# A decoder trunk in three blocks: where the sample group's expert rows are gathered, and who makes the weights' low parts

## The chip, the cores and the metric

The kernel runs on one core of one Trainium2 chip. The metric is the device time of one execution in microseconds; lower is better. The engines are named as the profile names them: PE is TensorE, DVE is VectorE, ACT is ScalarE, POOL is GpSimd, SP is SyncE, which here only issues transfers.

## What is computed

One layer of a decoder, for a prompt of 1024 rows and a sample group of 64 rows (8 sequences of 8 steps), with the same weights for both. Cut to what matters:

```
xn = RMSNorm(x)
lru_x, lru_gate, q, k, v, gate_lru, gate_attn = split(xn @ w_in)
A = (RG-LRU(conv4(lru_x)) * gelu(lru_gate)) @ w_branch_lru
B = window_attention(norm(q), norm(k), v) @ w_branch_attn
h = x + (sigmoid(gate_lru) * A + sigmoid(gate_attn) * B) @ w_out
y = h + PEER(RMSNorm(h))
```

PEER chooses, for each row, 8 heads x 16 experts of 16384 (the best sums of two lists of 128 key scores). An expert e is one row u[e] and one row v[e] of 1024 numbers each: the result is the sum over the 128 chosen experts of gelu(x . u[e]) * g[e] * v[e], with g a softmax of the scores.

## The kernel before

**Blocks.** The rows pass through the trunk in three blocks, called here by the number that the code gives them: block 0 is prompt rows 0 to 255 and the sample group, block 1 is prompt rows 256 to 639, block 2 is prompt rows 640 to 1023. `trunk` runs one block: the query, key and value columns (`qkv`, which makes columns 4 and 0 of the next block ahead of time), `attention`, a first merge of eight steps (`w_branch_attn`), the recurrent stage (`lru`, six calls), a second merge of eight steps (`w_branch_lru`), the output columns (`w_out`, four calls), the second norm, and `retrieve`, which makes the query columns and the 16 best keys of each list (16 calls).

**Weights in two parts.** Every weight is used as a sum of a high part (the fp32 value rounded to TensorE's fp32r) and a low part (what is left), and three matmuls make one product (`mm3`, L183 to L185). The weights come in 84 chunks of 128 x 1024 numbers (0.524 MB) and are loaded anew in each block. For each chunk ACT writes the high part into `whi` and DVE subtracts it for the low part, `wlo` (`split`, L163 and L164). `wsplit` (L201) counts the uses of a chunk. At the first use, in block 0, POOL sends the low part to memory (`lo_d`, L213). At the second the low part is subtracted again. At the third, SP reads it back (L209) and nothing is subtracted. There are three `whi`, three `wlo` and three `wraw` buffers, and SP's transfers are issued in one order: what stands behind a transfer that waits for a buffer waits too.

**Work in the background.** What follows a block's retrieval is a generator, `behind(b)`, that the next block's trunk advances: `bg(n)` takes n steps from it, and the tuples PG1 (while block 1 runs) and PG2 (while block 2 runs) say how many at each kind of call. Their eight entries belong to the first merge, the recurrent stage, the second merge, the output columns, the norm, the query columns, the q/k/v columns, and the score groups of attention. At the end of a block `bg(1000)` takes all that is left. A background is made of three kinds of steps:

- *choice steps* (`choose`): for each 128 rows, the best of the pairs of keys, the experts' numbers and the softmax, on DVE; the sample group comes first, and its experts' numbers and weights go to the small buffer `est` (L851);
- *gather steps*, for the sample group alone: its 64 rows x 128 experts are laid out as 128 partitions x 64 slots. `early_u` gathers one u row a partition for a slot (POOL, L963) and multiplies it by x (DVE, L965); after 64 slots comes a gelu. `early_v` gathers v rows (L978) and adds them up (L983); then the two halves and the residual are added, and the sample group's y is written;
- *g building* (`build_g`): for each 4 rows a 128 x 128 table of weights, as a product of two one-hot tables (DVE L940 and L941, ACT L943, PE L923), copied by ACT into `sg` (L924); 8 steps fill one `sg`, and SP writes it (L926). Block 0 has 64 such steps, block 1 has 96.

In the loop of `behind`, each step takes one choice step and, once the sample group's choice is there and attention is past, one gather step: of u behind block 0 (while block 1 runs), of v behind block 1 (while block 2 runs). g building comes after both.

**One large buffer.** Attention's keys and values (`at`), the gathers (`et`: x or the sum, and three rows) and g building's `sg` are all tiles of one tag, `at`, that has a single buffer. A tile takes it when the one before has been used for the last time.

**Order.** The program is written out in the order of the code, and a planner then places the instructions on each engine by the order of the code and by when it reckons them ready, so background work is interleaved with the trunk's and can run later, or a little earlier, than its place in the code.

After the blocks comes the expert loop for prompt rows (`dense`), which takes more than half of the time and is not touched.

Of the kernel before, what the change touches and what calls it, by code (L numbers as in the profile page):

```python
# [58 lines left out]
NR = 3  # L59
GBL = 1  # L60
PG0 = (0, 0, 0, 0, 0, 0, 0, 0)
PG1 = (5, 5, 4, 5, 2, 2, 0, 0)
PG2 = (6, 6, 5, 1, 2, 4, 2, 2)
LATE = 3
VJ = 1
EARLY = (4, 0)
# [4 lines left out]
def f32(ap):  # L71
    return ap.bitcast(F32)


class Kern:
# [125 lines left out]
    def wsplit(self, key, hi, lo, raw):  # L201

        nc = self.nc
        m = self.chunk.setdefault(key, len(self.chunk))
        use = self.uses[key] = self.uses.get(key, 0) + 1
        kept = self.lo_d[m].rearrange("p (k c) -> p k c", c=raw.shape[2])
        if use == 3:
            nc.scalar.copy(hi, raw)
            nc.sync.dma_start(f32(lo), kept)  # L209
            return  # L210
        self.split(hi, lo, raw)
        if use == 1:
            nc.gpsimd.dma_start(kept, f32(lo))  # L213

    def load_c(self, src, c0):

# [79 lines left out]
    def trunk(self, bi, x, raw, bg):  # L296
# [4 lines left out]
        xh, xl = x  # L301
        self.pg = (PG0, PG1, PG2)[bi]
        self.at_free = False
# [688 lines left out]

    def behind(self, b):

        early, left = None, True
        ch = self.choose(b)
        while left or early is not False:
            if early is None and self.es is not None and self.at_free:
                early = self.early_v() if b else self.early_u()
            if left:  # L1000
                left = next(ch, None) is not None
            if early and next(early, None) is None:
                early = False
            yield True
        for _ in self.build_g(b):
            yield True
# [203 lines left out]
```

## Time and profile before

| what | value |
|---|---|
| runs | 3771.19 us median of 3 (3761.95 to 3776.55) |
| the profiled execution | 3777.02 us; its span, from the first to the last instruction, 3775.2 us |
| mean granted TensorE clock of that execution | 0.945 of full speed |
| PE, DVE, ACT, POOL busy | 3401.7, 2889.4, 1453.8, 1539.4 us |

The profile is of one execution, and times in it are microseconds from the start of its span. A PE that is busy is not PE at its peak, since matmuls overlap; the time of a stage is read from the stretch between its first and last instruction, and its limit from the engine that is full there or from what the others wait for.

### The profile page before, as it was taken

How to read it: one execution, taken by the hardware profiler on the slowest of the kernel's cores; microseconds unless marked ns; L12 is line 12 of the kernel's file. 1: busy time of each engine (PE TensorE's matmuls, PEld its weight loads, DVE VectorE, ACT ScalarE, POOL GpSimd, SP SyncE). 2: the span in 40 equal slices, each digit the busy share in tenths (PEclk: the TensorE clock that was granted, in tenths of full speed). 3: DMA queues.
4: the chain of work that ended last, by engine and by line, in shares of the span. 5: the costliest groups of instructions: out<-in, count | busy, mean ns of one | idle time of the engine just before them, and what ended most of it. 6: DMA issues, size and time to landing. Idle time of an engine off the chain costs nothing. (4 is left out here: it accounts for less than half of the span.)

```text
span 3775.2 us, 59354 instructions
## 1 busy us (share of the span) xinstructions
PE 3401.7 (90%) x21891; PEld 3244.8 (86%) x21891; DVE 2889.4 (77%) x6727; ACT 1453.8 (39%) x2969; POOL 1539.4 (41%) x1240
## 2 busy tenths in 40 slices
PE   6898999868898998769779999999999999999996
PEld 6798978758795887668679999999999999999995
DVE  6567797998689975546999777777777776778777
ACT  4555345445854473676222222222222222222220
POOL 0011100340000222000367676767667776777774
PEclk8899999879998999889789999999999999999998
DMA  7388833776552899645478898989989899899897
GB/s 229 108 260 283 264 97 96 242 231 220 183 187 69 272 320 344 238 159 199 162 259 285 314 311 289 312 298 321 311 298 319 307 316 312 310 320 318 310 310 276
DMA packets 539235, 968.36 MB, mean 257 GB/s; under 512 B 38108, under 2 KB 356508, under 8 KB 535840
## 3 DMA queue, kind: packets, MB, share of 16 engines
q0 software_dynamic: 141120, 513.86, 38.1%
q1 hardware_dynamic: 397824, 450.70, 37.5%
q8 instruction: 172, 2.82, 0.3%
q14 instruction: 119, 0.97, 0.1%
HBM read 860.10 MB, written 105.99 MB: 256 GB/s over the span
## 5 line engine op out<-in xcount | busy, mean ns | idle before, releaser
L183 PE MATMUL ou<-ah,vh 128*128 128x256 f32 (+1 forms) x2048 | 637.0, 315 | 58.7 <-DVE dac L1078 30.5
L183 PE MATMUL sc<-dx,uh 128*128 128x256 f32 (+1 forms) x2048 | 636.6, 311 | 11.0 <-DMA gt<-g_d 8.7
L185 PE MATMUL sc<-dx,ul 128*128 128x256 f32 (+1 forms) x2048 | 635.4, 311 | 1.3 <-POOL ul L164 1.3
L184 PE MATMUL sc<-dx,uh 128*128 128x256 f32 (+1 forms) x2048 | 636.2, 311 | 0.0
L184 PE MATMUL ou<-al,vh 128*128 128x256 f32 (+1 forms) x2048 | 632.0, 311 | 3.5 <-DVE al L164 3.2
L185 PE MATMUL ou<-ah,vl 128*128 128x256 f32 (+1 forms) x2048 | 630.3, 310 | 2.5 <-POOL vl L164 2.5
L903 DVE SCALAR_TENSOR_TENSOR acc<-row,hv,acc 128x1024 f32<-128x1024 f32 x384 | 493.6, 1285 | 147.7 <-DMA row<-in_expert_v,iA 145.5
L891 DVE SCALAR_TENSOR_TENSOR row<-row,xt 128x1024 f32<-128x1024 f32 x384 | 464.9, 1216 | 133.6 <-DMA row<-in_expert_u,iA 126.3
L889 POOL DMA_INDIRECT row<-in_expert_u,iA x384 | 366.4, 954 | 279.5 <-DVE row L891 193.2
L901 POOL DMA_INDIRECT row<-in_expert_v,iA x384 | 360.8, 940 | 273.3 <-DVE acc L903 189.9
L183 PEld LDWEIGHTS ou<-ah,vh 128*128 128x128 f32 x2048 | 387.5, 190 | 77.9 <-DVE dac L1078 40.3
L164 POOL TENSOR_TENSOR ul<-un,uh 128x1024 fp32r<-128x1024 f32 x128 | 308.0, 2406 | 330.2 <-DMA gt<-g_d 303.4
L183 PEld LDWEIGHTS sc<-dx,uh 128*128 128x128 f32 x2048 | 392.0, 191 | 12.2 <-ACT uh L163 9.0
L184 PEld LDWEIGHTS ou<-al,vh 128*128 128x128 f32 x2048 | 389.3, 190 | 6.0 <-DVE al L164 5.4
L185 PEld LDWEIGHTS sc<-dx,ul 128*128 128x128 f32 x2048 | 390.9, 191 | 2.1 <-POOL ul L164 2.1
L184 PEld LDWEIGHTS sc<-dx,uh 128*128 128x128 f32 x2048 | 391.9, 191 | 0.0
L185 PEld LDWEIGHTS ou<-ah,vl 128*128 128x128 f32 x2048 | 388.4, 190 | 2.7 <-POOL vl L164 2.7
L1078 DVE TENSOR_TENSOR dac<-dac,ou 128x384 f32<-128x384 f32 (+1 forms) x672 | 314.9, 482 | 46.0 <-PE ou L185 44.9
L163 ACT CAST uh<-un 128x1024 fp32r<-128x1024 f32 x128 | 134.5, 1051 | 496.3 <-PE sc L184 366.7
L164 POOL TENSOR_TENSOR vl<-vn,vh 128x1024 fp32r<-128x1024 f32 x128 | 308.9, 2419 | 16.0 <-ACT vh L163 14.3
L978 POOL DMA_INDIRECT et<-in_expert_v,est x64 | 71.6, 1119 | 585.0 <-DVE oi L940 389.6
L183 PE MATMUL mm<-xh,whi 128*128 128x384 f32 (+1 forms) x768 | 260.1, 339 | 20.1 <-ACT Ti L687 16.8
(294 smaller groups left out, 7655.8 us busy)
## 6 DMA issues: line engine op xcount, KB each, us to landing
wraw<-in_w_in SPq DMA_DIRECT2D x132, 512.0 KB
un<-in_expert_uT SPq DMA_DIRECT2D x128, 512.0 KB
vn<-in_expert_v SPq DMA_DIRECT2D x128, 512.0 KB
lo_d<-wlo POOLq DMA_DIRECT2D x84, 512.0 KB, 5.9
wlo<-lo_d SPq DMA_DIRECT2D x84, 512.0 KB
g_d<-sg SPq DMA_DIRECT2D x20, 2048.0 KB
wraw<-in_peer_w_query SPq DMA_DIRECT2D x48, 512.0 KB
gt<-g_d SPq DMA_DIRECT2D x32, 768.0 KB
```

The lines of the kernel that those rows point to most:

```text
L163: nc.scalar.copy(hi, src)
L164: return (lo_eng or nc.vector).tensor_tensor(lo, src, f32(hi), op=ALU.subtract)
L183: nc.tensor.matmul(ps, lh, rh, start=first and j == 0, stop=False)
L184: nc.tensor.matmul(ps, lh, rl, start=False, stop=False)
L185: nc.tensor.matmul(ps, ll, rh, start=False, stop=last and j == n - 1)
L889: nc.gpsimd.indirect_dma_start(out=row, out_offset=None, in_=i["expert_u"], in_offset=bass.IndirectOffsetOnAxis(ap=ia[:, s:s + 1], axis=0))
L891: nc.vector.scalar_tensor_tensor(row, row, 1.0, xt, op0=ALU.mult, op1=ALU.mult, accum_out=hv[:, s:s + 1])
L901: nc.gpsimd.indirect_dma_start(out=row, out_offset=None, in_=i["expert_v"], in_offset=bass.IndirectOffsetOnAxis(ap=ia[:, s:s + 1], axis=0))
L903: nc.vector.scalar_tensor_tensor(acc, row, hv[:, s:s + 1], acc, op0=ALU.mult, op1=ALU.add)
L978: nc.gpsimd.indirect_dma_start(out=row(s), out_offset=None, in_=self.i["expert_v"], in_offset=bass.IndirectOffsetOnAxis(ap=self.es[:, 0, s ...
L1078: nc.vector.tensor_tensor(ac[k // 4][:, k % 4, a:b], ac[k // 4][:, k % 4, a:b], ps[:, 0:b - a], op=ALU.add)
```

## The change

There are three edits.

- `wsplit`: the low part of a chunk is read back at the second use as well as at the third, and sent to memory at the first, as before.
- `behind`: while block 1 runs, the gather steps are those of u and then those of v, two in each step of the loop; while block 2 runs there are none.
- PG1 and PG2: in block 1 the first merge takes 6 steps a call instead of 5. In block 2 the first merge and the recurrent stage take 5 instead of 6, the second merge 4 instead of 5, the output columns 3 instead of 1, the query columns 2 instead of 4, the q/k/v columns 2 as before, the score groups 1 instead of 2, and the norm 2 as before.

```diff
@@ -59,8 +59,8 @@
 NR = 3
 GBL = 1
 PG0 = (0, 0, 0, 0, 0, 0, 0, 0)
-PG1 = (5, 5, 4, 5, 2, 2, 0, 0)
-PG2 = (6, 6, 5, 1, 2, 4, 2, 2)
+PG1 = (6, 5, 4, 5, 2, 2, 0, 0)
+PG2 = (5, 5, 4, 3, 2, 2, 2, 1)
 LATE = 3
 VJ = 1
 EARLY = (4, 0)
@@ -204,13 +204,12 @@
         m = self.chunk.setdefault(key, len(self.chunk))
         use = self.uses[key] = self.uses.get(key, 0) + 1
         kept = self.lo_d[m].rearrange("p (k c) -> p k c", c=raw.shape[2])
-        if use == 3:
+        if use > 1:
             nc.scalar.copy(hi, raw)
             nc.sync.dma_start(f32(lo), kept)
             return
         self.split(hi, lo, raw)
-        if use == 1:
-            nc.gpsimd.dma_start(kept, f32(lo))
+        nc.gpsimd.dma_start(kept, f32(lo))
 
     def load_c(self, src, c0):
 
@@ -992,15 +991,16 @@
 
     def behind(self, b):
 
-        early, left = None, True
+        early, left = False if b else None, True
         ch = self.choose(b)
         while left or early is not False:
             if early is None and self.es is not None and self.at_free:
-                early = self.early_v() if b else self.early_u()
+                early = itertools.chain(self.early_u(), self.early_v())
             if left:
                 left = next(ch, None) is not None
-            if early and next(early, None) is None:
-                early = False
+            for _ in range(2):
+                if early and next(early, None) is None:
+                    early = False
             yield True
         for _ in self.build_g(b):
             yield True
```

## Rows read from the trace of the kernel before

**Rows 1.** The page, busy time by engine: busy us (share of the span) xinstructions.

```profile
PE 3401.7 (90%) x21891; PEld 3244.8 (86%) x21891; DVE 2889.4 (77%) x6727; ACT 1453.8 (39%) x2969; POOL 1539.4 (41%) x1240
```

**Rows 2.** Busy time by stretch: us, PE, PEld, DVE, ACT, POOL (x), PEclk, DMA share, GB/s.

```profile
490.00:531.00 41.00, 34.40 (x256) 31.30 (x255) 40.02 (x211) 14.52 (x27) 0.00 (x0) 0.88 0.31 91
531.00:604.00 73.00, 65.70 (x348) 45.51 (x347) 61.37 (x155) 52.75 (x164) 0.00 (x0) 0.95 0.08 22
604.00:671.00 67.00, 67.00 (x371) 65.08 (x370) 52.71 (x162) 20.86 (x30) 0.00 (x0) 1.00 0.49 147
671.00:817.00 146.00, 104.31 (x485) 90.84 (x483) 141.60 (x296) 73.74 (x110) 61.64 (x51) 0.82 0.80 252
817.00:884.00 67.00, 60.94 (x321) 59.02 (x321) 62.41 (x175) 29.28 (x56) 17.96 (x14) 0.94 0.72 224
...
1126.00:1250.00 124.00, 104.03 (x524) 75.42 (x523) 122.25 (x528) 68.86 (x197) 0.00 (x0) 0.85 0.29 92
1250.00:1319.00 69.00, 65.20 (x358) 62.06 (x357) 64.56 (x155) 22.27 (x37) 17.64 (x16) 1.00 0.98 326
1319.00:1424.00 105.00, 95.70 (x510) 87.58 (x508) 84.42 (x137) 75.81 (x125) 29.07 (x26) 0.98 0.96 315
1424.00:1491.00 67.00, 59.80 (x318) 57.91 (x318) 31.07 (x39) 19.64 (x26) 19.66 (x17) 0.95 1.01 338
...
1543.00:1678.00 135.00, 83.59 (x537) 77.47 (x538) 76.93 (x173) 116.18 (x335) 0.00 (x0) 0.80 0.46 174
```

**Rows 3.** The `et` buffer by tile, 650 to 880: xcount, ns min/median/max, first and last start.

```profile
L963 POOL DMA_INDIRECT et<-in_expert_u,est x64: 935/1074/1989, 675.2 to 863.3; - x64
L965 DVE SCALAR_TENSOR_TENSOR et<-et x64: 1173/1219/1229, 680.2 to 871.4; 128x1024 f32<-128x1024 f32 x64
...
DMA to landing us min/median/max: 4.2/5.2/8.7
```

**Rows 4.** The `sg` buffer by tile, 900 to 1130, and SP's line of time, 1112 to 1128.

```profile
L924 ACT COPY sg<-tr x64: 563/586/610, 922.3 to 1118.4; 128x512 f32<-128x512 f32 x64
...
1119.01 0.34 SPq L926 DMA_DIRECT2D g_d<-sg  x1
...
1126.63 0.57 SPq L417 DMA_DIRECT2D at<-kcar_d  x1
```

**Rows 5.** The `et` buffer by tile, 1250 to 1545.

```profile
L978 POOL DMA_INDIRECT et<-in_expert_v,est x64: 934/1009/2214, 1254.8 to 1520.8; - x64
L983 DVE SCALAR_TENSOR_TENSOR et<-et,eh x63: 1236/1279/1286, 1266.0 to 1526.2; 128x1024 f32<-128x1024 f32 x63
...
DMA to landing us min/median/max: 4.2/7.1/11.2
```

**Rows 6.** The `sg` buffer by tile, 1540 to 1680.

```profile
L924 ACT COPY sg<-tr x64: 558/586/610, 1543.9 to 1673.5; 128x512 f32<-128x512 f32 x64
```

**Rows 7.** The chosen indices `est` by tile, 600 to 700.

```profile
L851 SPq DMA_DIRECT2D est<-ft x4: 468/542/590, 645.3 to 671.1; - x4
```

**Rows 8.** The low parts `wlo` by tile, 657 to 1160.

```profile
L164 DVE TENSOR_TENSOR wlo<-wraw,whi x58: 1198/1218/1229, 655.9 to 1091.7; 128x1024 fp32r<-128x1024 f32 x58
```

**Rows 9.** DMA queues and issues, 657 to 1160: packets, MB, share; and xcount, KB each.

```profile
q1 hardware_dynamic: 75120, 70.95, 43.9%
q0 software_dynamic: 9216, 33.56, 20.2%
...
g_d<-sg SPq DMA_DIRECT2D x8, 2048.0 KB
```

**Rows 10.** Busy time by stretch, block 2's transfers and its whole remainder.

```profile
1255.00:1345.00 90.00, 86.20 (x491) 83.71 (x490) 82.74 (x184) 31.88 (x55) 25.38 (x23) 1.00 1.05 352
1250.00:1543.00 293.00, 257.80 (x1472) 243.63 (x1470) 201.73 (x360) 128.92 (x202) 71.60 (x64) 0.96 0.97 324
1250.00:1820.00 570.00, 462.68 (x2728) 434.63 (x2726) 373.29 (x968) 314.44 (x708) 71.60 (x64) 0.90 0.73 249
```

**Rows 11.** Query columns of block 1, by line, 1000 to 1130.

```profile
L764 ACT COPY qr<-mm x16: 457/474/482, 1029.5 to 1121.7; 128x384 f32<-128x384 f32 x16
```

## The prediction, made before the changed kernel ran

> **What bounds the kernel now.** I read the page first [rows 1]: TensorE is busy 90% of the span, but over half of the span is the expert loop at the end, which the diff does not touch. So I cut the first 1820 us into stages with the view of busy time by stretch and looked for the engine that is full in each [rows 2]. The reader is to see four different limits there. In the first merge of block 1 (604 to 671) TensorE is full. In its recurrent stage (671 to 817) VectorE is full, 141.6 of 146 us, and TensorE has only 104. In the same stages of block 2 (1250 to 1491) neither is full, but the DMA engines are, at 0.96 to 1.01. And from 1543 to 1678 ScalarE is the busiest: there g building runs almost alone.
>
> Then I followed one buffer by name, the `at` buffer, of which there is one. Attention, the gathers for the sample group (`et`) and g building (`sg`) take it in turn, and the views by tile give its diary. In block 1 the gathers of u hold it from 675.2 to 872.6, first issue to end of the last product, which is 3.08 us a row over 64 rows [rows 3]. Then 64 copies of g building fill it until 1118.4; its last write is issued at 1119.0, and block 2's attention sends its first transfer into it at 1126.6 [rows 4]. So attention already waits for this buffer, and for nothing longer. In block 2 the gathers of v hold it from 1254.8 to 1527.5, 4.26 us a row [rows 5], and g building follows as one lump, 64 copies from 1543.9 to 1673.5, 130 us [rows 6]. The queries of block 2 come after the lump, because its steps stand ahead of them in the order.
>
> **The change part by part.** *The v gathers move from block 2 to block 1.* Their order stays: u, then v, then g building, one `at` at a time. So block 1's diary becomes: first gather, 128 rows instead of 64, a closing sum, the lump, attention of block 2. Each link costs:
>
> First gather: it waits for the sample group's chosen indices, the last of which are sent at 671.1 [rows 7]. Six low-part subtractions of 1.217 us [rows 8] go from 490 to 531, where VectorE is full (40.0 of 41 us): 7 to 8 us. Sixteen go from the first merge, where VectorE is busy 52.7 of 67 us; they bring the choice forward by something between nothing and 19 us, and I take 10, as VectorE is neither full nor idle there. So 675 becomes 657.
>
> Pace: the two ends are the rows themselves, 3.08 us (beside it one stream of weights) and 4.26 us (beside it two, high parts and low parts, as block 1 will have). A gather takes 5.2 us from issue to landing in the one, 7.1 in the other [rows 3, 5], and `et` has room for three rows. The middle is 3.67: 128 x 3.67, and 10 us to drain u before v (a landing, a product and the gelu), make 480. The bytes say nearly the same. From 657 to 1160 the queues carried 71.0 and 33.6 MB, of which eight g writes, 16.8 MB, will come after the gathers [rows 9]; 58 subtractions there [rows 8] become reads of 0.524 MB, 30.4 MB; v adds 33.6. These are 152 MB, and at the 324 GB/s of 1250 to 1543 [rows 10] they take 468 us. I take 475: the last v row is done at 1132. The ends are 404 us (u's pace) and 555 (v's pace).
>
> After the last row: 16 us to the first g copy (1527.5 to 1543.9), 130 for the lump, 7 for its last write [rows 4 to 6]. `at` is free at 1285 instead of 1126. The trunk of block 1, whose last query columns are copied at 1121.7 now [rows 11], is done long before that, so no work of its own covers the wait; all that follows reads keys and values in `at`.
>
> Attention of block 2 took 124 us, 1126 to 1250, with choice steps in it and VectorE full (122.3). Block 1's, without steps, took 73 [rows 2]. The choice and the q columns can run during the wait, so I take 73, and 9 for the keys: the merge starts at 1285 + 82 = 1367 instead of 1250, **+117 us**.
>
> *What block 2 gets back.* 1250 to 1820 are 570 us, with TensorE busy 463, VectorE 373, ScalarE 314 [rows 10]. Without the v gathers the DMA engines are no longer full, and `at` is free when the merge begins, so the lump of 1543 to 1678 dissolves into the 5, 4 and 3 steps a call. TensorE's work stays, so 463 is the floor. Where TensorE was not held up for a whole stage it was busy about 0.91 (60.9 of 67 us at 817 to 884, 95.7 of 105 at 1319 to 1424 [rows 2]): 463 / 0.915 = 506, a gain of 64 us. The ends are 475 (hardly a gap) and 535 (half of the gain).
>
> *Low parts read instead of subtracted.* In block 1's weights 84 subtractions of 1.217 us, 102 us of VectorE, go. Each becomes a read of 512 KB that SP issues after a wait for one of three low buffers, with the next weight load queued behind it. In the recurrent stage VectorE is full and 19 of them, 23 us, are on the path, so the trunk gets faster there. But the trunk no longer sets the end of block 1, the diary does; I count nothing for them beyond the 18 us at the first gather, and the wait for `at` is what hides the rest. If that cover were gone they would bring 23 us more. The price of the reads is in the pace.
>
> *Steps.* Two gather steps a call let u and v begin and end in the list where u alone did; the three rows in `et` set the pace, not the list. Fewer steps in block 2's attention and queries, and more in its output stage, are counted in the 82 and the 506.
>
> The sum is +117 - 64 = **+53 us** on the profiled execution's 3777.0 (its span is 3775.2). The median of the runs is 3771.2, 0.15% less, so I expect 3824.
>
> **Where a rule and a row differ.** The pace is the disputed term. The highest rate that lasted here is 352 GB/s, from 1255 to 1345 [rows 10]; with it the 152 MB take 431 us, the last v row is done at 1088, and the sum is +73 - 64 = +9. The Trainium skill ("DMA: Bandwidth & Descriptors", section "Bandwidth") gives 425 GB/s for one core alone with 16 MB transfers; as an estimate by that page the bytes would take 357 us and be no limit. No row here shows such a rate over a stage.
>
> **The rivals.** *A, faster.* The transfers have room, and both lists go at u's 3.08 us a row: the last v row is done at 657 + 404 = 1061, `at` is free at 1214, the merge starts at 1296, +46. With block 2 at 475 the sum is 46 - 95 = -49, 3722; with 506 it is -18. It decides if the last v row comes before about 1070. For it: a landing of 7.1 us and a product of 1.3 us, three rows at a time, would permit 2.8 us a row. Against: in block 2 the pace was 4.26 although VectorE had time to spare (31 of 67 us busy at 1424 to 1491). Chance 0.20. The rate that the Trainium skill's page gives would make this rival the likeliest.
>
> *B, no change.* 352 GB/s hold all through block 1, as worked out above: 3780. For it: the transfers of 1255 to 1345 were of these same kinds. Against: it held for 90 us, and only 324 over the whole stretch. Chance 0.17.
>
> *C, worse than forecast.* V's 4.26 us for both lists: the last row at 1212, +197 - 64, 3904. For it: block 1 will have just that traffic. Against: its recurrent stage, short of VectorE, asks for weights more slowly. It is the upper part of the forecast, which with it has 0.63.
>
> **Numbers.** Forecast 3824. Its own range is 3790 to 3890; to hold the time 8 times in 10 it takes in B and the milder half of A, and leaves out the ends of A and C: 3742 to 3890. A measurement of this kernel can tell about 0.5%, 19 us, from no change. Faster 0.20, same 0.17, slower 0.63.
>
> **What would show it.** Right: gathers of v from about 890 to 1130, in block 1; no low-part subtraction in the recurrent stage, and that stage shorter; block 1's g copies as one lump of 130 us that ends near 1280, with TensorE idle around it and block 2's first scores after it; no lump in block 2. Wrong: block 1's g copies well under way before 1070, block 2's scores at 1130 to 1200, or a block 2 that still takes 570 us from its merge on.

## The result, and the profile after

| what | before | after |
|---|---|---|
| median of 8 runs | 3775.19 us (3761.95 to 3776.55) | 3801.96 us (3787.81 to 3807.42) |
| ratio | 1 | 1.0072, 95% interval 1.0056 to 1.0088 |
| the profiled execution's span | 3775.2 us | 3800.6 us |
| mean granted TensorE clock | 0.945 | 0.943 |

The change costs 27 us, 0.7%. The forecast was 3824. In the rows below a line number of the changed kernel is one less than in [rows 3 to 6] (L923 is L924 there).

The page, busy time by engine; it answers to [rows 1]:

```profile
PE 3353.9 (88%) x21891; PEld 3216.4 (85%) x21891; DVE 2794.4 (74%) x6643; ACT 1451.3 (38%) x2971; POOL 1523.3 (40%) x1240
```

TensorE is busy 48 us less with as many instructions, and VectorE 95 us less with 84 fewer, and yet the kernel takes longer: the cost is a wait.

The `et` buffer by tile, in the changed kernel; it answers to [rows 3, 5]. Columns as there.

```profile
L962 POOL DMA_INDIRECT et<-in_expert_u,est x64: 932/940/1682, 649.2 to 893.6; - x64
L964 DVE SCALAR_TENSOR_TENSOR et<-et x64: 1200/1218/1268, 654.9 to 904.4; 128x1024 f32<-128x1024 f32 x64
L977 POOL DMA_INDIRECT et<-in_expert_v,est x64: 932/937/1915, 905.9 to 1047.1; - x64
L982 DVE SCALAR_TENSOR_TENSOR et<-et,eh x63: 1283/1285/1289, 912.3 to 1052.8; 128x1024 f32<-128x1024 f32 x63
...
  ACT sg L923: 156.8, 1
```

The reader is to see v's gathers in block 1, right behind u's. First gather to last product, u takes 649.2 to 905.5, 4.00 us a row, and v takes 905.9 to 1054.1, 2.32 us a row. The last line, from the part on who waited for this buffer, is one wait of ScalarE, of 156.8 us.

The `sg` buffer by tile, block 1's stretch and then block 2's, and the load into `at` (line L416); they answer to [rows 4, 6].

```profile
L923 ACT COPY sg<-tr x64: 562/586/612, 1062.6 to 1239.0; 128x512 f32<-128x512 f32 x64
...
  DMA out_y<-et: 156.8, 1
```

```profile
L923 ACT COPY sg<-tr x96: 561/586/616, 1467.7 to 1793.7; 128x512 f32<-128x512 f32 x96
```

```profile
L416 SPq DMA_DIRECT2D at<-kcar_d x1: 572/572/572, 1247.2 to 1247.2; - x1
```

Block 1's g building is one lump of 176 us behind the v gathers, and `at` comes free at 1247.2 instead of 1126.6 (before). In block 2 the 96 copies are spread over 326 us: no lump any more.

Busy time by stretch, changed kernel; it answers to [rows 2, 10]: us, PE, PEld, DVE, ACT, POOL (x), PEclk, DMA share, GB/s.

```profile
662.00:786.00 124.00, 106.16 (x519) 96.85 (x520) 115.36 (x286) 78.27 (x120) 32.56 (x31) 0.92 0.91 300
786.00:848.00 62.00, 57.02 (x325) 55.40 (x325) 47.49 (x99) 31.63 (x66) 14.96 (x15) 0.97 1.05 362
848.00:906.00 58.00, 35.67 (x275) 35.05 (x274) 27.13 (x53) 10.97 (x13) 15.81 (x15) 0.82 0.97 351
906.00:1062.00 156.00, 0.00 (x0) 0.00 (x0) 84.26 (x67) 0.00 (x0) 63.58 (x64) 0.50 0.72 220
1062.00:1247.00 185.00, 152.26 (x1027) 147.67 (x1028) 110.31 (x374) 133.48 (x346) 0.00 (x0) 0.90 0.57 199
1247.00:1371.00 124.00, 112.89 (x675) 91.85 (x673) 122.86 (x561) 65.79 (x173) 0.00 (x0) 0.93 0.38 122
1371.00:1845.00 474.00, 440.66 (x2785) 424.39 (x2785) 305.78 (x955) 325.26 (x748) 0.00 (x0) 0.96 0.70 232
```

From 906 to 1062 TensorE and ScalarE do nothing at all. Only the gathers of v go on, at 220 GB/s. The recurrent stage is shorter (124 us instead of 146), and block 2's remainder has TensorE busy 0.93 of the time, where it was 0.81 [rows 10].

What stood still there is told by the waits of 900 to 1070 (us in total, times, longest) and ScalarE's line of time (in brackets: idle before it, and what released it).

```profile
PEld tr L922 <- ACT sg L923: 175.2, 1, 175.2
PE tr L922 <- ACT sg L923: 175.0, 1, 175.0
ACT sg L923 <- DMA out_y<-et: 156.8, 1, 156.8
```

```profile
905.63 0.26 ACT L966 ACTIVATE eh<-eh 128x64 f32<-128x64 f32 x1 [12.92 <-DVE et L964]
1062.64 1.56 ACT L923 COPY sg<-tr 128x512 f32<-128x512 f32 x3 [156.76 <-DMA out_y<-et]
```

The first g copy stands in ScalarE's queue right behind u's gelu. It needs `sg`, so it waits until the sample group's y has left `et`. Behind it in the same queue stand block 1's norm and its query columns, which have nothing to do with `at`; TensorE's transposes of g building wait for the copies, and the trunk's matmuls behind them. So the background's wait parked the whole trunk. The Trainium skill ("Perfetto Trace Analysis", section "Tensor Engine Instruction (MATMUL, LD_WEIGHTS)") says that the execution queues of ScalarE, VectorE and GpSimd are strictly first in, first out, and that TensorE's can only pull weight loads ahead; this trace agrees, with not one ScalarE instruction in 156.8 us.

### The profile page after: what moved, and what is told of

Read it like the earlier page. It is cut to its first block, busy times and chain, and to the rows that moved or that the text cites. A ratio compares the mean times of both kernels' runs of the same rounds, so it can differ in the third digit from the quotient of the medians.

```text
span 3800.6 us, 59357 instructions
## 1 busy us (share of the span) xinstructions
PE 3353.9 (88%) x21891; PEld 3216.4 (85%) x21891; DVE 2794.4 (74%) x6643; ACT 1451.3 (38%) x2971; POOL 1523.3 (40%) x1240
## 4 chain that ended last, share of the span: by engine, by line
PE 25%; DMA 19%; DVE 12%; issue 7%; POOL 7%; ACT 5%; POOLq 0%; DVEq 0%; ACTq 0%
DMA row<-in_expert_v,iA 7%; DMA row<-in_expert_u,iA 4%; DMA et<-in_expert_v,est 3%; PE ou L183 3%; PE ou L184 3%; PE ou L185 3%; PE mm L183 3%; PE mm L185 3%; PE mm L184 3%; DVE row L890 3%; POOL row L888 2%; DMA vn<-in_expert_v 2%; PE tr L922 2%; POOL vl L164 2%; PE sc L183 2%
## 5 line engine op out<-in xcount | busy, mean ns | idle before, releaser
L183 PE MATMUL ou<-ah,vh 128*128 128x384 f32 (+1 forms) x2048 | 636.4, 315 | 58.3 <-ACT ah L163 33.6
L184 PE MATMUL ou<-al,vh 128*128 128x384 f32 (+1 forms) x2048 | 631.1, 310 | 0.9 <-DVE al L164 0.5
L922 PE MATMUL tr<-oij 128*128 128x128 f32 x1280 | 179.1, 293 | 211.9 <-ACT sg L923 208.1
L922 PEld LDWEIGHTS tr<-oij 128*128 128x128 f32 x1280 | 172.0, 207 | 218.7 <-ACT sg L923 211.7
```

The source lines that it names most:

```text
L183: nc.tensor.matmul(ps, lh, rh, start=first and j == 0, stop=False)
L184: nc.tensor.matmul(ps, lh, rl, start=False, stop=False)
L922: nc.tensor.matmul(pt[:, x, :], oj[:, x], wi[:, x], start=True, stop=True)
```

## Experiments

Two theories stood after the result. *The diary*: one buffer, taken in turn by the gathers, g building and attention, sets when block 2 can begin, so the time follows the moment when `at` comes free. *The parked queue*: the 156 us in which the trunk stood still are the cost, and a later first g copy would bring them back. The steps list and the traffic of the low parts were the other suspects. Each kernel was timed beside the kernel before on the same chip; ratios are to that. Where two changed kernels are compared, it is by their medians, which were taken at different times; by the ratios these differences come out up to 9 us smaller.

**One part of the change at a time, and the change without one.**

`e1_read_only`, on the kernel before:

```diff
-        if use == 3:
+        if use > 1:
...
-        if use == 1:
-            nc.gpsimd.dma_start(kept, f32(lo))
+        nc.gpsimd.dma_start(kept, f32(lo))
```

> The kernel before with only the low parts read back at the second use. Diary theory (the turn of u, v and g building in the one large buffer sets the end of block 1): v stays in block 2, so nothing like +27 us. Block 1's recurrent stage gets shorter than 146 us, but u's rows go at about 4.0 us instead of 3.08, so the buffer comes free about 20 to 40 us later than 1126; the two nearly cancel: 3765 to 3795. Rival, the reads (43 MB more to move) are what costs: about 3800, with the whole loss here.

Measured: 3756.99 us, ratio 0.9958 (0.9942 to 0.9974). The reads alone gain 16 us. The `et` buffer's products and the load of `at`, by tile and by line:

```profile
L964 DVE SCALAR_TENSOR_TENSOR et<-et x64: 1175/1219/1272, 659.5 to 902.0; 128x1024 f32<-128x1024 f32 x64
```

```profile
L416 SPq DMA_DIRECT2D at<-kcar_d x1: 572/572/572, 1101.3 to 1101.3; - x1
```

u ends 30 us later than in [rows 3], since beside the reads it goes at 3.92 us a row; but the trunk is ahead, g building starts at 903.4 instead of 922.3, and `at` is free 25 us earlier. The time is below the range expected of it, and the buffer comes earlier where it was expected later.

`e2_gather_only`, on the kernel before: the edit of `behind` as in the change, nothing else.

```diff
-        early, left = None, True
+        early, left = False if b else None, True
...
-                early = self.early_v() if b else self.early_u()
+                early = itertools.chain(self.early_u(), self.early_v())
...
-            if early and next(early, None) is None:
-                early = False
+            for _ in range(2):
+                if early and next(early, None) is None:
+                    early = False
```

> The kernel before with only u and v both gathered in block 1, two steps a call; low parts subtracted at the second use, old steps a call. Diary theory: the large loss of block 1 and the gain of block 2 are both here: the buffer free at 1220 to 1260, no lump in block 2, 3785 to 3825. Rival, the reads cost and the move itself gains: faster than before, 3740 to 3765.

Measured: 3813.05 us, 1.0101 (1.0081 to 1.0121). The move alone costs 40 us, and `at` comes free at 1258.4.

`e3_steps_only`, on the kernel before:

```diff
-PG1 = (5, 5, 4, 5, 2, 2, 0, 0)
-PG2 = (6, 6, 5, 1, 2, 4, 2, 2)
+PG1 = (6, 5, 4, 5, 2, 2, 0, 0)
+PG2 = (5, 5, 4, 3, 2, 2, 2, 1)
```

> The kernel before with only the new steps a call. Diary theory: the buffer's turns set the times, not the list of steps: within 0.5% of before, 3755 to 3795, and block 2's lump of 130 us still stands. Rival, spreading the steps is what dissolves the lump: the lump is gone and 40 us or more are gained.

Measured: 3774.22 us, 1.0007 (0.9994 to 1.0020): nothing. The stretch of block 2's lump:

```profile
1540.00:1680.00 140.00, 85.08 (x524) 80.78 (x523) 67.34 (x169) 97.63 (x268) 0.00 (x0) 0.78 0.47 169
```

TensorE is busy 85 of 140 us, much as in the lump before (83.6 of 135, [rows 2]). While v holds the buffer until about 1546 (the sample group's y leaves `et` at 1546.3), another list can't spread a lump that waits for it. What the list did change gained nothing: the last search of block 2 comes at 1793.4 instead of 1816.4, but the g copies run until 1818.1 (1784.9 before), and the expert loop begins at 1830.0 (1825.1 before).

`e4_no_read`, on the changed kernel: low parts subtracted at the second use, as before.

```diff
-        if use > 1:
+        if use == 3:
...
-        nc.gpsimd.dma_start(kept, f32(lo))
+        if use == 1:
+            nc.gpsimd.dma_start(kept, f32(lo))
```

> The changed kernel with the low parts subtracted again at the second use. Diary theory: u goes faster (3.1 to 3.5 us a row instead of 4.0) but the choice comes later and the recurrent stage is longer; the buffer free within 30 us of 1247, 3785 to 3825. Rival, the reads cost: back to 3775 or under.

Measured: 3793.84 us, 1.0055 (1.0039 to 1.0072). With the v gathers in block 1 the reads no longer gain; the interval overlaps that of the whole change. u starts at 678.3 instead of 649.2 but takes 3.03 us a row instead of 4.00, and `at` is free at 1238.1: the early start that the reads bring is spent on slower gathers. Against `e2_gather_only` it also shows that the new steps list, worth nothing alone, gives some 19 us (3813.05 to 3793.84) once v is out of block 2's way; in the two traces the expert loop begins 9 us earlier (1857.5 and 1848.6). The parts alone, -0.42, +1.01 and +0.07%, add up to +0.66%, near the measured +0.72%, but only because these two interactions nearly cancel.

**The parked queue.** `e5_g_late`, on the changed kernel: fewer background steps before the queries, so that g building begins later in the order.

```diff
-PG1 = (6, 5, 4, 5, 2, 2, 0, 0)
+PG1 = (6, 5, 1, 0, 0, 4, 0, 0)
```

> The changed kernel with block 1's g steps listed later: 6, 5, 1, 0, 0, 4 steps at the merge, recurrent, second merge, output, norm and query calls, so that g building stands behind the second norm in the order. Queue theory (ScalarE was parked 157 us on the first g copy, and the norm and the queries behind it stood still): they now run while v is gathered, v goes slower (3 to 4 us a row instead of 2.3), the buffer comes free at 1200 to 1260, and attention of block 2 no longer shares its time with the queries: 3750 to 3785. Rival, the buffer alone sets the end and what the trunk does meanwhile is free: 3790 to 3815.

Measured: 3816.84 us, 1.0128 (1.0102 to 1.0154), slower than the change itself. The waits of 900 to 1110:

```profile
ACT sg L923 <- DMA out_y<-et: 133.2, 1, 133.2
```

Part of the query columns now ran, 922 to 950 (6 of 16 copies); then the first g copy parked ScalarE again for 133 us, v's last row came at 1088.5, and `at` was free at 1269.0, 22 us later. Attention, with fewer queries beside it, then took 100 us to the first tanh of the merge instead of 124. So what the trunk gained there the buffer's later turns took back: the merge begins at 1368.7 (1371.3 in the change) and the expert loop at 1850.1 (1853.4). From where the median has its further 15 us the trace doesn't show. This theory fell in the form that I had given it: the stall is real, but a later place in the list didn't remove it. Nor does its length order the times: ScalarE was parked 90 us in `e2_gather_only` (3813.05), 91 in `e4_no_read` (3793.84), 133 here and 157 in the change (3801.96), while the order of the medians is that in which `at` comes free (1258.4, 1238.1, 1269.0, 1247.2), as far as it goes: neighbours' intervals overlap.

**The price of the v gathers.** `e6_no_v`, on the changed kernel. It leaves out v's gathers and their sum, so the sample group's y isn't written.

```diff
-                early = itertools.chain(self.early_u(), self.early_v())
+                early = self.early_u()
```

> The changed kernel without v's gathers and sum (the sample group's y is not written). Diary theory: the buffer comes free by v's whole 150 to 170 us sooner, at about 1085 to 1110, and as good as all of it shows in the end: 3650 to 3695. Rival, v is mostly beside other work: less than 60 us.

Measured: 3670.94 us, 0.9749 (0.9722 to 0.9776). The `sg` buffer by tile, block 1, and the load of `at`:

```profile
L923 ACT COPY sg<-tr x64: 558/586/603, 887.1 to 1024.5; 128x512 f32<-128x512 f32 x64
```

```profile
L416 SPq DMA_DIRECT2D at<-kcar_d x1: 524/524/524, 1033.9 to 1033.9; - x1
```

v in block 1 costs 131 us of the whole kernel (3801.96 less 3670.94), and it holds the buffer for 157 (905.5 to 1062.6). `at` comes free 213 us earlier, more than the 150 to 170 expected, since the lump is also shorter (137 us instead of 176) and u ends 19 us sooner. But here the buffer is no longer what block 2 waits for. Its scores, and the stretch after `at` is free:

```profile
L460 PE MATMUL mm<-at,qT x96: 376/376/792, 1146.7 to 1220.5; 64*128 64x256 f32 x96
```

```profile
1034.00:1130.00 96.00, 92.47 (x587) 91.62 (x587) 79.98 (x457) 32.50 (x51) 0.00 (x0) 0.98 0.76 246
```

The first scores come 113 us after `at` is free, and TensorE is busy 92.5 of the 96 us in between, with block 1's query columns (copied 1041.0 to 1117.1) among its work. The merge of block 2 begins at 1231.5, no earlier than in the kernel before (1232.2), where `at` came 93 us later. So this run prices the v gathers with all that they hold up, the buffer and the stopped trunk, and doesn't part the two. Its 100 us against the kernel before come from block 2 itself, which takes 471 us from the merge's first tanh to the last search instead of 584.

**Other places for the work.** `e7_v_last`: the kernel before with the reads, and v behind block 1's g building instead of ahead of it, in block 2.

```diff
-PG2 = (6, 6, 5, 1, 2, 4, 2, 2)
+PG2 = (6, 6, 5, 3, 2, 4, 2, 1)
...
-        early, left = None, True
+        early, left = False if b else None, True
...
-                early = self.early_v() if b else self.early_u()
+                early = self.early_u()
...
         for _ in self.build_g(b):
             yield True
+        for _ in self.early_v() if b == 1 else ():
+            yield True
```

> The kernel before with the low parts read back at the second use, and v gathered behind block 1 as before, but after block 1's g tables instead of ahead of them (6, 6, 5, 3, 2, 4, 2, 1 steps a call in block 2). Diary theory: block 1 as in the kernel with the reads only (attention's first transfer at about 1100), no lump in block 2 as g building has the buffer from the start of the merge, v from about 1560 to 1800 beside the output columns and the queries: 3690 to 3735. Rival, v's rows then end last and hold up the expert loop: 3760 to 3800.

Measured: 3759.38 us, 0.9968 (0.9948 to 0.9988). Stretches of block 2:

```profile
1250.00:1580.00 330.00, 307.78 (x2051) 298.79 (x2050) 198.91 (x445) 273.40 (x654) 0.00 (x0) 0.97 0.73 246
1731.00:1797.00 66.00, 0.00 (x0) 0.00 (x0) 40.42 (x90) 1.04 (x1) 19.67 (x21) 0.50 0.69 207
```

g building is spread and TensorE is busy 0.93 from 1250 to 1580. But v's last product comes at 1783, after the last search at 1731, and TensorE stands idle for 66 us ahead of the expert loop: the wait has moved to the end of block 2, as the rival said. Against `e1_read_only` (0.9958), which has the same reads, nothing is gained.

`e8_g_in_block2`, on the changed kernel: v stays in block 1, and block 0's g building moves to block 2.

```diff
-PG2 = (5, 5, 4, 3, 2, 2, 2, 1)
+PG2 = (6, 6, 5, 3, 2, 4, 2, 1)
...
-        for _ in self.build_g(b):
-            yield True
+        for bi in range(2) if b == 1 else ():
+            for _ in self.build_g(bi):
+                yield True
```

> The changed kernel with the g tables of block 0 built after the choice of block 1, in block 2, together with block 1's; block 1 then has only u and v in the large buffer (6, 6, 5, 3, 2, 4, 2, 1 steps a call in block 2, as there are 64 more). Diary theory: the lump of block 1, 176 us from the end of v to attention's first transfer in the changed kernel, is out of the buffer's way; the first transfer comes at 1060 to 1120 instead of 1247, block 2 gets 64 more g steps (50 to 110 us more from its merge on): 3680 to 3750. Rival, the trunk of block 1, which stood still, sets the end without the lump as well: 3780 to 3810.

Measured: 3733.62 us, 0.9904 (0.9886 to 0.9922): 36 us faster than the kernel before, 68 faster than the change, and the fastest full kernel here.

```profile
906.00:1060.00 154.00, 105.95 (x696) 104.76 (x694) 135.32 (x531) 36.58 (x53) 43.19 (x41) 0.86 0.95 317
1126.00:1204.00 78.00, 65.56 (x331) 46.24 (x332) 67.63 (x221) 52.06 (x160) 0.00 (x0) 0.85 0.11 34
1204.00:1773.00 569.00, 510.80 (x3292) 489.35 (x3290) 366.57 (x1052) 430.70 (x1061) 0.00 (x0) 0.95 0.66 224
```

With no g copy in ScalarE's queue, norm, queries and choice ran beside v (911 to 987 for the query columns), at a pace of v of 3.09 us a row, and `at` came free at 1126.7, as before the change and a little later than expected. The buffer is last here: TensorE stands idle until v's sum has left `et`, and the first thing that ScalarE then does is the copy of block 2's keys, for which it waited 99 us.

```profile
1060.00:1126.00 66.00, 0.00 (x0) 0.00 (x0) 43.80 (x88) 0.00 (x0) 22.98 (x23) 0.50 0.68 208
```

Attention then took 78 us, with little else beside it. Block 2's remainder, 569 us from the merge's first tanh to the last search, is shorter than before (584 on the same marks) although it holds 64 more g steps and none of them in a lump.

`e9_v_in_loop`, on the changed kernel: v's 64 gathers and their sum at the end of the expert loop's own list of gathers. The lines left out of the diff hold the sum, and the place in which the experts' numbers and weights are kept until then.

```diff
+        for s in range(NSLOT // 2):
...
+            nc.gpsimd.indirect_dma_start(out=row, out_offset=None, in_=i["expert_v"],
...
-                early = itertools.chain(self.early_u(), self.early_v())
+                early = self.early_u()
...
-            ngat = 2 * NSLOT * (NA // P)
+            ngat = 2 * NSLOT * (NA // P) + NSLOT // 2
```

> The changed kernel with v's gathers and sum moved out of the trunk altogether, into the expert loop behind the prompt's own 768 rows, with that loop's row buffers. Diary theory: the trunk is that of the kernel without v, whose expert loop starts at 1711 instead of 1853; the loop gets 64 gathers more on 768, 8%, where POOL, the vector engine and the transfers are busy 0.7 to 0.9, so between nothing and 80 us of the 131 are given back: 3672 to 3750. Rival, the loop is as full as the trunk and v costs there what it cost in block 1: 3790 to 3810.

Measured: 3797.04 us, 1.0062 (1.0044 to 1.0079).

```profile
3663.00:3797.00 134.00, 0.00 (x0) 0.00 (x0) 91.40 (x71) 2.02 (x2) 60.80 (x66) 0.50 0.81 272
```

The expert loop begins at 1732.2 instead of 1853.4, but the 64 gathers are left over when the last matmul is done and make a tail of 134 us. The time is the rival's. Spreading them over the loop wasn't tried, nor was a second large buffer for g building.

## Why the prediction was right, and where it was not

**The mechanism held where `at` is late.** Block 2 needs the buffer and a trunk that is done with block 1, and the traces tell which came last:

| kernel | `at` free | first tanh of block 2's merge | expert loop begins | median |
|---|---|---|---|---|
| before | 1126.6 | 1232.2 | 1825.1 | 3775.19 |
| `e1_read_only` | 1101.3 | 1209.1 | 1811.4 | 3756.99 |
| `e3_steps_only` | 1110.6 | 1233.5 | 1830.0 | 3774.22 |
| the change | 1247.2 | 1371.3 | 1853.4 | 3801.96 |
| `e2_gather_only` | 1258.4 | 1365.2 | 1857.5 | 3813.05 |
| `e4_no_read` | 1238.1 | 1362.5 | 1848.6 | 3793.84 |
| `e5_g_late` | 1269.0 | 1368.7 | 1850.1 | 3816.84 |
| `e6_no_v` | 1033.9 | 1231.5 | 1711.3 | 3670.94 |
| `e8_g_in_block2` | 1126.7 | 1204.2 | 1782.1 | 3733.62 |

In the four kernels with u, v and g building one behind the other in block 1, `at` comes free at 1238 to 1269 and the merge follows 100 to 124 us later; in `e8_g_in_block2` TensorE waits idle for it. That is the forecast's diary. But an early buffer doesn't bring block 2 forward by itself: in `e6_no_v` it is 93 us ahead of the kernel before, in `e3_steps_only` 16, and the merge begins within 1.3 us of where it did. The kernel before stood where both limits meet, with the last query columns of block 1 copied at 1121.7 [rows 11] and the buffer free at 1126.6: it waited for the buffer, as the prediction said, but the trunk's last copy was only 5 us sooner, and its searches ran until 1149.1. v in block 1, the lump behind it, TensorE idle ahead of it (for another reason than forecast), block 2's scores after it, and a block 2 without a lump all came.

**The two terms, on marks that both traces have** (first tanh of the merge of block 2, at 1232.2 before and 1371.3 after; last search of block 2, 1816.4 and 1844.9). Block 1's term is 139 us for a forecast of 117; block 2's gain is 139 - 28 = 111 for a forecast of 64. So the sum is 28 us instead of 53, because the gain was mis-sized. That the time came within 3790 to 3890 is in part luck: with the gain as measured and block 1's term as forecast, the sum would have been +6 us, or 3777. The step that failed in the gain is the floor of 463 us for TensorE's work, busy 0.915 (the two rows that it is taken from give 0.91, which makes 509 and a gain of 61). From the merge's first products with attention's low part to the last search, before and after:

```profile
1249.30:1816.40 567.10, 463.38 (x2730) 435.09 (x2728) 370.57 (x953) 314.44 (x708) 71.60 (x64) 0.90 0.73 251
1386.40:1845.00 458.60, 428.14 (x2730) 415.98 (x2728) 295.00 (x915) 312.69 (x710) 0.00 (x0) 0.96 0.72 238
```

The floor wasn't one: the same 2730 matmuls keep TensorE busy for 428 us instead of 463, and for 0.93 of the stretch. The 768 transposes for g building took 114.67 us before and 104.03 after, the 96 for the searches 27.4 and 19.3; before, 512 of the 768 ran in the lump, at a granted clock of 0.80 [rows 2], and the whole stretch was at 0.90; after, it was at 0.96. The products with weights took no less (84.0 and 84.1 us for the 245 with the low parts of `w_in`). So the clock is not all of the 35 us. The rest is not in the lengths of the instructions but in how they overlap: busy time counts overlapping matmuls once, and the groups of matmuls, 763 us before and 747 after when added up, differ by only 16. What of this the lump caused wasn't tested apart.

**Block 1's steps, one by one.** The near hit of its term is a sum of errors that cancel.

- First gather: forecast 657, measured 649.2. Right in kind.
- Pace: 475 us forecast, 405 measured (649.2 to 1054.1). This is rival A's 404, and the last row came before A's 1070. But A's pace came in two halves: u at 4.00, near the upper end, and v at 2.32, below both, because the trunk had stopped. With the trunk running beside it v took 3.09 (`e8_g_in_block2`). The reading behind the forecast, that in block 2 neither TensorE nor VectorE is full, is loose for the merge: 65.2 and 64.6 of 69 us at 1250 to 1319 [rows 2].
- "The trunk of block 1 is done long before that": wrong. It stood still from 906 to 1062, parked behind a g copy.
- The lump: 130 forecast, from block 2, where g building ran almost alone; 176 measured, with the delayed queries in it. [Rows 4] had the better measure, 196 us beside the queries.
- `at` free: forecast 1285, measured 1247.2, that is +121 instead of +158.
- Attention: 82 forecast, since queries and choice would be over; 124 measured to the merge's first tanh, since they weren't (query columns were copied until 1264.9). The 9 us for the keys had no row behind them; the first scores came 49 us after `at` was free, at 1296.5. VectorE is full in attention, 122.86 of 124 us. On the same marks it took 106 before, so +18 instead of -42.

**Reads and steps, counted at nothing.** Alone the reads gain 16 us, within the 23 that the prediction put beside them for a trunk without cover; behind the diary they gain nothing (`e4_no_read`). The recurrent stage did get 22 us shorter, without effect on the end. The steps list is worth nothing alone, and some 19 us beside the move.

**The disputed rate.** The highest rate over a stage in the changed kernel is 362 GB/s (786 to 848). The Trainium skill ("DMA: Bandwidth & Descriptors", section "Bandwidth") gives 425 GB/s for one core alone with 16 MB transfers; no run here shows it. Nor did the rate set v's pace: 220 GB/s in its stretch.

**What stays open.** How the 131 us of v in block 1, and the 68 us between the change and `e8_g_in_block2`, divide between the stopped trunk and the buffer. Taking v away, or g building out of block 1, ends both at once (and `e8_g_in_block2` has another steps list in block 2 as well), and `e5_g_late`, meant to part them, released only 28 us of the trunk's work.

## What to carry to other kernels

Where several kinds of background work take turns in one buffer, write down its diary (who holds it from when to when) and price a move by the moment at which the foreground gets it, not by the busy time of engines. Set beside it the moment at which the foreground would be ready: a buffer that is free before that gains nothing more (`e6_no_v`). Look also at which in-order queues the background's first waiting instruction will sit in: one copy that waits for a buffer holds back all foreground work behind it, and only taking it out of that stage helped here, not a later place in the list. A duration measured in a stage that ran alone, or at a lower granted clock, is not a floor for the same work elsewhere.

## What the runs showed that was not expected

The pace of row gathers was put down to the transfers, and by the waits it mostly wasn't theirs. Who waited for `et` while v was gathered in block 2 of the kernel before, in us and times, stands under its tile's view, 1250 to 1545:

```profile
  POOL et L978: 181.5, 53
  DVE et L983: 9.7, 6
```

With three rows of room, GpSimd waited for products 181.5 us and VectorE for landings 9.7: the products were late, behind other work of VectorE, which in part waited itself (33.1 us for matmuls, at L338). How far the full DMA engines slowed that other work isn't shown. In the changed kernel the same gathers, with little else on VectorE, took 2.32 us a row although one landed 5.1 us after its issue. That is near what three in flight allow, as an estimate from these rows: (5.1 + 1.3) / 3 = 2.1. In the other direction, u's pace went from 3.08 to 4.00 us a row when reads of 512 KB took the place of subtractions, with a landing of 7.5 us instead of 5.2. Even there GpSimd's wait for products grew more, from 85.7 to 128.7 us, than VectorE's for landings, from 8.2 to 22.5.

TensorE, idle from 906 to 1062, was granted 0.50 in that stretch, the level of 1.2 GHz; the next, 1062 to 1247, shows 0.90, and the work after 1371 0.96. So the stop of 156 us is followed by a higher granted clock than that of the lump before the change, 0.80 with TensorE busy 83.6 of 135 us [rows 2].
